# Decoder step on one core: the first projection's tiles, identity products, and the order of weight loads at the output projection

## The chip, the core and the metric

The kernel runs on one core of one Trainium2 chip. The metric is the device time of one execution in microseconds (us), the median of the runs; smaller is better. TensorE does the matrix products (and its weight loads beside them), VectorE (DVE), ScalarE (ACT) and GpSimd (POOL) the elementwise work, SyncE (SP) issues the transfers.

## What is computed

One inference step of a decoder with two layers and width 1024, over a prompt of 2048 tokens and 32 sample tokens (8 sequences of 4) with a paged cache. Layer 0 has an HGRN2 branch (heads "A") and a forgetting-attention branch (heads "B"), layer 1 is GLA (heads "C"). Cut to what matters here:

```python
def rmsnorm(x, g):
    xf = x.astype(jnp.float32)
    y = xf * lax.rsqrt(jnp.mean(xf * xf, axis=-1, keepdims=True) + EPS)
    return (y * g.astype(jnp.float32)).astype(x.dtype)
...
def even_mixer(h, w_in, b_fox, lb, hgrn_gain, w_out, hgrn_s0, fox_attend):
    proj = h @ w_in
    qa, fa, ia, ga, qb, kb, vb, gb, fb = _split(proj, [A_WIDTH] * 4 + [B_WIDTH] * 4 + [B_HEADS])
    ...
    out = jnp.concatenate([o_a, o_b], axis=-1) @ w_out
    return out, s_a, kb_h, vb_h, log_fb
```

The change touches two places of this: `rmsnorm` with `h @ w_in` for the first rows of the prompt, and `... @ w_out` of layer 0.

## The kernel before

Every f32 product is made of f16 halves: an operand is split into a hi and a lo part, and one product is three matrix products, hi by hi, hi by lo and lo by hi (`mm3`, L476 to L480). The prompt goes in two halves of 1024 rows; the first half also carries the 32 sample rows, so it has eight tiles of 128 tokens and one of 32.

**Units of weights.** A projection is cut into units of up to 272 columns of weights. A unit has four steps (`half_unit`, L315): *fetch* loads the raw weights (tiles `wr_*`), *measure* takes the largest absolute value of each of four parts on VectorE (tiles `rm_*`, L292, L294), *scale* spreads it over the partitions with a product against the identity on TensorE (tile `spr_*`, L279) and makes a power of two of it on VectorE, *split* makes the hi and lo weights (`w_*`; ScalarE L345 and L352, VectorE L346, GpSimd L353). `staged` (L1070) calls the products of unit j and, between them, steps of units j+1 to j+3, by a list `todo`. The first unit of layer 0 is "Ai" (values v, products `pt_Av`, tokens on the partitions, 48 products for a pair of tiles), the second "Ag" (gates, products `pf_Ag`, in segments of 352 tokens of 24 products each), the third "Aqf".

**Ahead of the first unit's products** stands the norm (`norm_groups`, L408), for pairs of token tiles. *prep* squares a tile with the sum on ScalarE (L426, `nsq`), takes the mean and its root (VectorE L403 `rst`, GpSimd L405) and scales the tile on VectorE (L428, `nx`). *turn* transposes eight pieces k = 0 to 7 of both tiles on TensorE (L440, `nt`), and `split_evac` evacuates each piece as hi on ScalarE (L473) and lo on VectorE (L474) into `act`. A product of piece k needs both. `handover` (L452) interleaves the pairs' turns with the products of the first unit; in the first half `turn1` prepares pairs 2 and 3. The sample tile's products are a form of their own (`few_rows`, L510): copies `sam` on VectorE (L517), products `pS` (L522), three additions on VectorE (L527). The constants of later steps (`more_consts`) follow on VectorE.

**The order on an engine** is decided when the program is built, by a scheduler; `tc.issue_after(x)` keeps the instructions in its scope behind x. At run time each engine works through its list in order and waits by semaphores.

**The start of the output projection** (`phase_odd`, L1798): the rows y of layer 0 come back from memory in pieces of 256 tokens (`y_pieces`, L1608, tiles `yr`, two buffers), are split into `act` (ScalarE L1628 to L1632, VectorE L1633, GpSimd L1630), and meet four units of weights (`wr_o`, called units 0 to 3 here, products `pt_o`); `row_tiles` (L1859) loads the rows of x that are added.

Notation: L12 is line 12 of the kernel before; `nx_512` is the tile of tokens 512 to 639.

Of the kernel before, what the change touches and what calls it, by code (L numbers as in the profile page):

```python
# [1 line left out]

# [119 lines left out]
class Kern:  # L122
# [134 lines left out]
    def spread(self, x, pps, tag, nm):  # L257

        nc = self.nc
        m, t = self.kcol(), self.kcol()  # L260
        nc.vector.tensor_reduce(m, x, mybir.AxisListType.X, ALU.max, apply_absolute_value=True)
        ps = pps.tile([P, 512], F32, tag=tag, name=f"spr_{nm}")
        nc.tensor.matmul(ps[:, :P], m.to_broadcast([P, P]), self.ident, start=True, stop=True)
        nc.vector.reduce_max(t, ps[:, :P], axis=mybir.AxisListType.X)
        return t
# [141 lines left out]

    def norm_groups(self, pool, pps, act, hf, get_tile, gain, tags=("gr", "o")):  # L408

        nc = self.nc
        tiles = self.ttiles(hf)

        def mk(grp):
            xs, raw = [], []

            def load():
                raw.extend(get_tile(c0, n) for c0, n in grp)

            def prep():
                for j, (c0, n) in enumerate(grp):
# [8 lines left out]
            def turn(at=None, then=None):  # L431
                c0 = grp[0][0]
                if grp[-1][0] == HALF:
                    self.sam = None
                with ExitStack() as st:
                    for k in range(KT):
                        ps = pps.tile([P, 512], F32, tag=tags[k % 2], name=f"nt{c0}_{k}")
                        w = 0
                        for (_, n), xn in zip(grp, xs):
                            nc.tensor.transpose(ps[:, w : w + n], xn[:n, k * P : (k + 1) * P], self.ident[:n, :n])  # L440
                            w += n
                        self.split_evac(ps[:, :w], act[0][:, k, c0 : c0 + w], act[1][:, k, c0 : c0 + w],
                                        gain[:, k : k + 1])
                        if k == at:
                            then(st)

            return prep, turn, load

        return [mk(tiles[g : g + 2]) for g in range(0, len(tiles), 2)]
# [32 lines left out]
    def proj_fm(self, pps, act, W, off, M, hf, evac, nm):  # L482
        for c0, n in self.segs(hf):
            ps = pps.tile([P, 512], F32, tag="pj", name=f"pf_{nm}{c0}")
            for k in range(KT):
                self.mm3(ps[:M, :n], [x[:, k, off : off + M] for x in W],
                         [x[:, k, c0 : c0 + n] for x in act], k == 0, k == KT - 1)
            evac(ps[:M, :n], c0, n)
            yield 24 * (n / 2.4 + 3)

    def proj_tm(self, pps, act, W, hf, evac, nm, width=256, pairs=True):
# [3 lines left out]
        for g in range(0, len(tl), per):  # L495
# [7 lines left out]
            for j, (c0, n) in enumerate(grp):  # L503
                for k in range(KT):
                    self.mm3(ps[:n, j], [x[:, k, c0 : c0 + n] for x in act],
                             [x[:, k, :width] for x in W], k == 0, k == KT - 1)
            evac(ps[:n, : len(grp)], g, len(grp), n)
# [450 lines left out]
    def phase_even(self):  # L958
# [4 lines left out]
        with pool("act", side="right") as ap, pool("w", side="right") as w0, pool("wl", side="right") as wp1, \  # L963
# [30 lines left out]
            for hf in range(2):  # L994
# [10 lines left out]
                lin = lins[hf]  # L1005
                groups = self.norm_groups(nrm, pps, act, hf, get_x, self.g_even)
                first = self.handover(groups, dense(0, 1), last)
                if hf == 0:
# [19 lines left out]
                    turns = [turn0, turn1] + [g[1] for g in groups[2:]]  # L1028
                    first = self.handover(list(zip(steps, turns)), dense(0, 1), last)
                    drain(first)  # L1030
                    with tc.issue_after(self.last_x.ins), tc.issue_after(self.last_a.ins), \
                            tc.issue_after(self.last_v.ins):
                        self.more_consts(wp)
# [36 lines left out]
    def staged(self, us, a, b, beside=None):  # L1070
# [537 lines left out]
    def y_pieces(self, hf, layer, act, pool):  # L1608
# [5 lines left out]
        def mk(c0, dc, s, w, sy):  # L1614
            t = {}

            def load():
                t["raw"] = pool.tile([P, KT, 256], F32, tag="yr", name=f"yr{layer}{hf}{c0}{s}")[:, :, :w]
                nc.sync.dma_start(t["raw"], y[:, :, dc + s : dc + s + w].rearrange("k p t -> p k t"))

# [177 lines left out]
    def phase_odd(self):  # L1798
# [4 lines left out]
        with pool("act2", side="right") as ap, pool("w2", side="right") as w0, pool("yr2", side="right") as y0, \  # L1803
# [197 lines left out]
```

## Time and profile before

| | us |
|---|---|
| median of 3 runs | 2395.92 |
| lowest and highest run | 2392.24, 2399.04 |
| profiled execution | 2394.72 |
| its span in the trace | 2392.4 |
| TensorE busy in it | 2294.1 |
| VectorE, ScalarE, GpSimd busy | 1417.9, 1107.5, 753.7 |

The profile shows one execution. The device time holds the span and 2.3 us around it. The granted TensorE clock was 0.986 of full speed on average. TensorE is busy nearly throughout; the stretches that the change touches are the first 75 us and some 40 us from 1300 us on.

### The profile page before, as it was taken

The page shows a single profiled execution, that of the slowest core. Times are in us where ns is not written, and L with a number is a line of the kernel's source. Part 1 is how long each engine was busy: PE and PEld are TensorE (multiplying, and loading weights), DVE is VectorE, ACT ScalarE, POOL GpSimd, SP SyncE. Part 2 cuts the span into 40 slices and gives each one's busy share as a digit, 9 for nine tenths or more (in the row PEclk, how much of TensorE's full clock was granted, in tenths as well). Part 3 has the DMA queues.
Part 4 walks back from the last instruction along what each step waited for, and adds up shares of the span by engine and source line. Part 5 has one row for each costly group of instructions (what it writes and reads, how often), then busy time and mean ns, then how long its engine had stood idle before and what let it go on. Part 6 is the DMA issues. An engine that isn't in the chain of part 4 may idle for free. (4 is left out here: it accounts for less than half of the span.)

```text
span 2392.4 us, 58667 instructions
## 1 busy us (share of the span) xinstructions
PE 2294.1 (96%) x23324; PEld 1633.7 (68%) x23324; DVE 1417.9 (59%) x3347; ACT 1107.5 (46%) x2458; POOL 753.7 (32%) x843
## 2 busy tenths in 40 slices
PE   6999999999999999999999999999999999999998
PEld 5677677864655875655446876777778766666887
DVE  7566556446655548666767463665675645557554
ACT  5334343342333226556667454535543635545333
POOL 2233222112212225234556211432452222322322
PEclk9999999999999999999999999999999999999999
DMA  6231234535541267676874632122156312114453
GB/s 198 63 88 58 81 113 142 175 92 143 149 136 43 85 192 258 223 251 203 270 241 134 213 109 58 46 81 86 50 151 196 111 41 70 43 59 159 154 192 147
DMA packets 297013, 317.24 MB, mean 133 GB/s; under 512 B 39730, under 2 KB 241011, under 8 KB 296739
## 3 DMA queue, kind: packets, MB, share of 16 engines
q1 hardware_dynamic: 295234, 308.98, 41.1%
q8 instruction: 183, 3.00, 0.5%
q0 software_dynamic: 1504, 4.52, 0.5%
q14 instruction: 92, 0.75, 0.1%
HBM read 242.31 MB, written 71.11 MB: 131 GB/s over the span
## 5 line engine op out<-in xcount | busy, mean ns | idle before, releaser
L480 PE MATMUL pt_o<-w_o,act 128*128 128x256 f16 x1024 | 280.5, 274 | 3.1 <-DVE act L1633 2.9
L478 PE MATMUL pt_o<-w_o,act 128*128 128x256 f16 x1024 | 280.7, 274 | 1.3 <-ACT sg1C L534 1.1
L479 PE MATMUL pt_o<-w_o,act 128*128 128x256 f16 x1024 | 280.5, 274 | 1.0 <-POOL w_o L353 1.0
L480 PEld LDWEIGHTS <-act 128*128 128x128 f16 x2304 | 226.6, 98 | 36.1 <-issue 4.6
L478 PEld LDWEIGHTS <-act 128*128 128x128 f16 x2304 | 226.6, 98 | 36.0 <-ACT act L473 4.0
L479 PEld LDWEIGHTS <-act 128*128 128x128 f16 x2304 | 226.7, 98 | 32.4 <-issue 2.9
L478 PE MATMUL pt_Cv<-w_Cv,act 128*128 128x256 f16 (+1 forms) x512 | 140.3, 275 | 1.7 <-ACT act L473 0.9
L644 POOL TENSOR_TENSOR kA<-kA,fA 128x512 f32<-128x512 f32 (+1 forms) x56 | 79.8, 1425 | 192.6 <-PE gl_A L610 143.0
L479 PE MATMUL pt_Cv<-w_Cv,act 128*128 128x256 f16 (+1 forms) x512 | 140.0, 274 | 0.0
L480 PE MATMUL pt_Cv<-w_Cv,act 128*128 128x256 f16 (+1 forms) x512 | 139.7, 274 | 0.0
L1241 ACT ACTIVATE L<-L,nm,kc 128x512 f32<-128x512 f32 (+3 forms) x160 | 118.2, 741 | 36.9 <-DVE nm L1239 27.2
L644 POOL TENSOR_TENSOR kC<-kC,fC 128x512 f32<-128x512 f32 (+1 forms) x56 | 81.8, 1461 | 148.2 <-PE gl_C L610 101.3
L1249 POOL TENSOR_SCALAR L<-L,nm 128x512 f32<-128x512 f32 (+3 forms) x160 | 98.8, 631 | 70.8 <-DVE nm L1245 28.6
L1276 ACT ACTIVATE th<-pt 128x512 f16<-128x512 f32 (+3 forms) x159 | 80.7, 527 | 59.8 <-PE pt L1269 58.9
L1277 DVE TENSOR_TENSOR tl<-pt,th 128x512 f16<-128x512 f32 (+3 forms) x159 | 94.4, 609 | 20.3 <-ACT th L1276 19.0
L1269 PE MATMUL pt<-ident,L 128*128 128x128 f32 x544 | 91.3, 280 | 4.9 <-DVE tl L1277 2.4
L1269 PEld LDWEIGHTS pt<-ident,L 128*128 128x128 f32 x544 | 66.7, 143 | 32.4 <-DVE tl L1277 9.1
L1393 PEld LDWEIGHTS pkt<-ident,pgcache_fox_k 128*128 128x128 f32 x512 | 58.1, 141 | 44.4 <-issue 25.6
L1393 PE MATMUL pkt<-ident,pgcache_fox_k 128*128 128x128 f32 x512 | 76.1, 279 | 4.7 <-DVE kts L1397 2.0
L478 PE MATMUL pt_Av<-w_Ai,act 128*128 128x256 f16 x256 | 70.9, 277 | 1.9 <-ACT act L473 1.9
L479 PE MATMUL pt_Av<-w_Ai,act 128*128 128x256 f16 x256 | 70.7, 276 | 0.4 <-DVE w_Ai L346 0.4
L478 PE MATMUL pt_Bk<-w_Bk,act 128*128 128x256 f16 x256 | 71.0, 277 | 0.0
(952 smaller groups left out, 6738.3 us busy)
## 6 DMA issues: line engine op xcount, KB each, us to landing
pgcache_fox_k<-in_cache_fox_k SPq DMA_DIRECT2D x128, 256.0 KB, 4.2
pgcache_fox_v<-in_cache_fox_v SPq DMA_DIRECT2D x128, 256.0 KB, 4.2
yr<-yT SPq DMA_DIRECT2D x16, 1024.0 KB, 7.4
nx<-in_x_prompt SPq DMA_DIRECT2D x16, 512.0 KB, 5.4
wr_Aqf<-in_w_in_even SPq DMA_DIRECT2D x64, 128.0 KB, 3.2
wr_o<-in_w_out_even SPq DMA_DIRECT2D x32, 256.0 KB, 4.5
wr_Cv<-in_w_in_odd SPq DMA_DIRECT2D x32, 256.0 KB, 3.8
wr_Cqk<-in_w_in_odd SPq DMA_DIRECT2D x64, 128.0 KB, 2.8
```

The lines of the kernel that those rows point to most:

```text
L478: nc.tensor.matmul(ps, lh[0], rh[0], start=first, stop=False)
L479: nc.tensor.matmul(ps, lh[0], rh[1], start=False, stop=False)
L480: return nc.tensor.matmul(ps, lh[1], rh[0], start=False, stop=last)
L644: nc.gpsimd.tensor_tensor(kv[:, :, 0], kv[:, :, 0], t1.to_broadcast([P, nb, w]), ALU.mult)
L1241: self.last_exp = nc.scalar.activation(lt[:, :w], lt[:, :w], AF.Exp, bias=nm[:, 0:1], scale=ib, accum_out=nm[:, 2 + j : 3 + j])
L1249: nc.gpsimd.tensor_scalar(lt[:, :w], lt[:, :w], nm[:, 1:2], 2.0**14, ALU.mult, ALU.mult)
L1269: nc.tensor.transpose(pt[:, w : w + P], rows[b][s // 4][0][:, (s % 4) * P : (s % 4 + 1) * P], self.ident)
L1276: nc.scalar.activation(th[:, a:w], pt[:, a:w], AF.Copy),
L1277: nc.vector.tensor_tensor(tl[:, a:w], pt[:, a:w], th[:, a:w], ALU.subtract)))
L1393: nc.tensor.transpose(pk[:, j * P : (j + 1) * P], pgs[j][:, h * P : (h + 1) * P], self.ident)
```

## The change

1. In the first half, the squares of the second tile of pairs 1 to 3 (tokens 384, 640 and 896) are made on VectorE, by one operation that multiplies and sums, and no longer on ScalarE.
2. 21 products of the identity with itself, 128x128 in f32 into a PSUM tile that nobody reads, are put ahead of and between the first pair's transposes: nine behind the gain's spread product, four behind the first transpose, one behind each of the eight transposes of the second tile.
3. Pair t+1 is loaded and prepared behind the middle of turn t, for t = 1 to 3; before, pairs 2 and 3 both in turn 1.
4. The first segment of the second unit is issued ahead of the sample rows' products of the first; the third unit is measured during the second instead of during the first, and its scale step is put behind the last product issued.
5. At the output projection, the row loads from the third on and the loads of units 2 and 3 stand behind the last piece of y.

```diff
+    def norm_groups(self, pool, pps, act, hf, get_tile, gain, tags=("gr", "o"), share=False):
...
-                    nc.scalar.activation(sq[:n], xt[:n], AF.Square, accum_out=ss[:n])
+                    if share and j and c0 > P:
+                        nc.vector.tensor_tensor_reduce(sq[:n], xt[:n], xt[:n], 1.0, 0.0, ALU.mult, ALU.add, ss[:n])
+                    else:
+                        nc.scalar.activation(sq[:n], xt[:n], AF.Square, accum_out=ss[:n])
...
+            warm = pps.tile([P, 512], F32, tag="st", name="warm")
+            def warm_up(n, after):
+                with tc.issue_after(after.ins):
+                    for _ in range(n):
+                        nc.tensor.matmul(warm[:, :P], self.ident, self.ident, start=True, stop=True)
+            warm_up(9, self.last_spread)
...
-                    def turn0():
-                        groups[0][1](1, lambda st: st.enter_context(tc.issue_after(self.last_scale.ins)))
-                    def turn1():
-                        groups[1][1](KT // 2 - 1, lambda st: behind(self.last_a, 2))
-                        behind(self.last_a, 3)
-                    steps = [lambda: None, lambda: behind(self.last_split, 1), lambda: None, lambda: None, groups[4][0]]
-                    turns = [turn0, turn1] + [g[1] for g in groups[2:]]
-                    first = self.handover(list(zip(steps, turns)), dense(0, 1), last)
+                    def each0(st, k, j):
+                        if j or k == 0:
+                            warm_up(1 if j else 4, self.last_t)
+                        if (k, j) == (2, 0):
+                            st.enter_context(tc.issue_after(self.last_scale.ins))
+                    def turn0():
+                        groups[0][1](each0)
+                    def turn(t):
+                        groups[t][1](lambda st, k, j: behind(self.last_a, t + 1) if (k, j) == (KT // 2, 0) else None)
+                    steps = [lambda: None, lambda: behind(self.last_split, 1), lambda: None, lambda: None, lambda: None]
+                    turns = [turn0] + [lambda t=t: turn(t) for t in (1, 2, 3)] + [groups[4][1]]
+                    first = dense(0, 1)
+                    drain(self.handover(list(zip(steps, turns)), islice(first, 4), last))
+                    gates = dense(1, 3)
+                    next(gates)
                     drain(first)
...
-                drain(dense(1, 3))
+                drain(dense(1, 3) if hf else gates)
...
+                    if n == 2:
+                        st.enter_context(self.tc.issue_after(self.last_mm.ins))
                     self.ready[u] = us[u][0][n]()
...
-            if j:
+            if j == 1 and beside:
+                todo = [[], [(2, 1), (4, 0)], [(2, 2)], [(2, 3), (3, 1)], [(3, 2)], [(3, 3)]]
+            elif j:
                 todo = [[(j + 3, 0), (j + 2, 1)], [(j + 2, 2)], [(j + 2, 3)]]
             elif beside is None:
                 todo = [[(2, 0), (1, 3)], [(3, 0)], [(2, 3)]]
             else:
-                todo = [[(1, 0)], [(1, 1)], [(2, 0), (1, 2), (1, 3)], [(3, 0)], [(2, 1), (2, 2), (2, 3)]]
+                todo = [[(1, 0)], [(1, 1)], [(2, 0), (1, 2), (1, 3)], [(3, 0)]]
...
-                    nc.sync.dma_start(t[:m], self.rows(hf, c0, m, first))
+                    with ExitStack() as st:
+                        if first and j > 1:
+                            st.enter_context(tc.issue_after(self.last_yr.ins))
+                        nc.sync.dma_start(t[:m], self.rows(hf, c0, m, first))
...
-            with tc.issue_after(self.last_y.ins):
+            with tc.issue_after(self.last_y.ins), tc.issue_after(self.last_yr.ins):
                 drain(dense(0, 3))
```

`last_mm`, `last_t`, `last_spread` and `last_yr` are the last such instruction issued. The changed file's line numbers lie some lines higher: its L478 and L477 are the lo and hi evacuations, L432 the scaling, L428 VectorE's square, L482 to L484 the three products.

**TensorE around the third unit's scale product.** `pS_Av` are the sample rows' products, `pf_Ag` the second unit's. Before:

```order
L522 MATMUL pS_Av_683<-w_Ai_153,sam_Av_680 32x256
L279 MATMUL spr_Aqf_721<-ident,rm_Aqf_715 128x128
L478 LDWEIGHTS w_Ag_577
L478 MATMUL pf_Ag_847<-act,w_Ag_577 128x352
L479 LDWEIGHTS w_Ag_577
```

After the change the scale product has left this place; in front of it stand three segments of the second unit, the first of them ahead of the sample rows' products:

```order
L484 MATMUL pf_Ag_913<-act,w_Ag_599 128x352
L280 MATMUL spr_Aqf_942<-ident,rm_Aqf_902 128x128
L482 LDWEIGHTS w_Ag_599
L482 MATMUL pf_Ag_951<-act,w_Ag_599 128x352
L483 LDWEIGHTS w_Ag_599
```

`pf_Ag_913` is the third segment and `pf_Ag_951` the fourth; before, all six came behind the first scale product.

**VectorE during pair 1's turn.** `act<-nt_k` is the lo evacuation of piece k, `rst` the mean of squares, `nx` the scaling of a tile. Before:

```order
L474 SCALAR_TENSOR_TENSOR act<-nt_3_241,g_even,act 128x256
L403 TENSOR_SCALAR rst_n_249<-nss_247 128x1
L428 TENSOR_SCALAR nx_512_166<-nx_512_166,rsr_n_251 128x1024
L474 SCALAR_TENSOR_TENSOR act<-nt_4_262,g_even,act 128x256
L261 TENSOR_REDUCE kc<-g_odd 128x1
L474 SCALAR_TENSOR_TENSOR act<-nt_5_267,g_even,act 128x256
L403 TENSOR_SCALAR rst_n_257<-nss_255 128x1
L474 SCALAR_TENSOR_TENSOR act<-nt_6_272,g_even,act 128x256
L428 TENSOR_SCALAR nx_640_168<-nx_640_168,rsr_n_259 128x1024
L474 SCALAR_TENSOR_TENSOR act<-nt_7_277,g_even,act 128x256
```

After:

```order
L478 SCALAR_TENSOR_TENSOR act<-nt_3_263,g_even,act 128x256
L404 TENSOR_SCALAR rst_n_273<-nss_271 128x1
L428 ISA nsq_278,nss_279<-nx_640_178 128x1024
L428 ISA nss_279 128x1
L478 SCALAR_TENSOR_TENSOR act<-nt_4_268,g_even,act 128x256
L262 TENSOR_REDUCE kc<-g_odd 128x1
L432 TENSOR_SCALAR nx_512_176<-nx_512_176,rsr_n_275 128x1024
L478 SCALAR_TENSOR_TENSOR act<-nt_5_289,g_even,act 128x256
L478 SCALAR_TENSOR_TENSOR act<-nt_6_294,g_even,act 128x256
L404 TENSOR_SCALAR rst_n_281<-nss_279 128x1
L478 SCALAR_TENSOR_TENSOR act<-nt_7_299,g_even,act 128x256
L432 TENSOR_SCALAR nx_640_178<-nx_640_178,rsr_n_283 128x1024
```

The square of tile 640 (the two rows `ISA`) stands behind the step that reads ScalarE's sum of tile 512, and ahead of the lo evacuation of piece 4.

**SyncE at the output projection.** `wr_o_19432` is unit 1, `wr_o_19542` and `wr_o_19611` are units 2 and 3; `yr` are the pieces of y of tokens 512, 768 and the sample rows. Before:

```order
L327 DMA wr_o_19432<-in_w_out_even 128x2x256 x4
L327 DMA wr_o_19542<-in_w_out_even 128x2x256
L1619 DMA yr_19437<-yT_76 128x8x256
L327 DMA wr_o_19542<-in_w_out_even 128x2x256 x3
L327 DMA wr_o_19611<-in_w_out_even 128x2x256 x4
L1619 DMA yr_19449<-yT_76 128x8x256
L1619 DMA yr_19461<-yT_76 128x8x32
```

After:

```order
L328 DMA wr_o_19454<-in_w_out_even 128x2x256 x4
L1646 DMA yr_19459<-yT_76 128x8x256
L1893 DMA row_0_19495<-in_x_prompt 128x1024
L1646 DMA yr_19471<-yT_76 128x8x256
L1893 DMA row_1_19497<-in_x_prompt 128x1024
L688 DMA s_C_21834<-in_state_gla 128x2x256
L688 DMA s_C_21836<-in_state_gla 128x2x256
L1646 DMA yr_19483<-yT_76 128x8x32
L1893 DMA row_2_19499<-in_x_prompt 128x1024
```

Seven more row loads follow there, and only then the eight loads of units 2 and 3.

## Rows read from the trace of the kernel before

**Rows 1.** Page, part 1: engine, busy us, share of the span, instructions

```profile
PE 2294.1 (96%) x23324; PEld 1633.7 (68%) x23324; DVE 1417.9 (59%) x3347; ACT 1107.5 (46%) x2458; POOL 753.7 (32%) x843
```

**Rows 2.** Waits of TensorE, 0 to 75 us: waiting line, releaser, total, times, longest

```profile
PE spr_Aqf L279 <- DVE kc L261: 6.8, 1, 6.8
PE nt L440 <- DVE nx L428: 5.2, 2, 3.8
PE pS_Av L522 <- DVE sam_Av L517: 1.5, 1, 1.5
```

**Rows 3.** Windows: length, busy (count) of PE, PEld, DVE, ACT, POOL, clock, DMA share, GB/s

```profile
52.40:59.10 6.70, 0.00 (x0) 0.00 (x0) 6.29 (x18) 0.98 (x2) 0.01 (x1) 0.50 0.48 145
59.10:64.00 4.90, 4.86 (x17) 2.79 (x18) 4.74 (x16) 0.32 (x3) 1.95 (x6) 0.50 0.00 0
```

**Rows 4.** Timeline of TensorE: start, duration, line, output and inputs

```profile
19.69 0.29 PE L480 MATMUL pt_Av<-w_Ai,act 128*128 128x256 f16 x1
...
23.71 0.28 PE L478 MATMUL pt_Av<-w_Ai,act 128*128 128x256 f16 x1
...
33.41 0.27 PE L478 MATMUL pt_Av<-w_Ai,act 128*128 128x256 f16 x1
...
41.87 0.27 PE L478 MATMUL pt_Av<-w_Ai,act 128*128 128x256 f16 x1
...
48.69 0.27 PE L480 MATMUL pt_Av<-w_Ai,act 128*128 128x256 f16 x1
...
72.68 0.31 PE L480 MATMUL pf_Ag<-act,w_Ag 128*128 128x352 f16 x1
72.83 0.31 PE L478 MATMUL pf_Ag<-act,w_Ag 128*128 128x352 f16 x1
...
83.57 0.31 PE L478 MATMUL pf_A00f<-act,w_Aqf 128*128 128x352 f16 x1
```

**Rows 5.** Timeline of ScalarE in the first pair of the first unit

```profile
23.18 1.57 ACT L473 ACTIVATE act<-nt,g_even 128x256 f16<-128x256 f32 x4 [4.12 <-PE nt L440]
24.62 1.07 ACT L426 ACTIVATE nsq<-nx 128x1024 bf16<-128x1024 f32 x1
...
25.66 0.85 ACT L817 ACTIVATE v<-pt_Av,kc 128x256 f32<-128x256 f32 x2
```

**Rows 6.** Timeline of VectorE, same stretch and ahead of it

```profile
17.69 0.88 DVE L474 SCALAR_TENSOR_TENSOR act<-nt,g_even,act 128x256 f16<-128x256 f32 x2
...
25.82 0.15 DVE L403 TENSOR_SCALAR rst_n<-nss 128x1 f32<-128x1 f32 x1 [0.47 <-ACT nsq L426]
...
29.20 0.75 DVE L428 TENSOR_SCALAR nx<-nx,rsr_n 128x1024 f32<-128x1024 f32 x1
29.87 0.48 DVE L474 SCALAR_TENSOR_TENSOR act<-nt,g_even,act 128x256 f16<-128x256 f32 x1
```

**Rows 7.** Tile views of fx and yr: durations ns min/median/max, first and last start, forms

```profile
L1829 DVE SCALAR_TENSOR_TENSOR fx<-fx,rsr_f,gb x9: 1272/1285/1286, 2305.4 to 2380.2; 128x1024 f32<-128x1024 f32 x8, 32x1024 f32<-32x1024 f32 x1
L1633 DVE SCALAR_TENSOR_TENSOR act<-yr,kc,act x54: 275/746/1986, 1294.5 to 2311.9; 128x512 f16<-128x512 f32 x48, 128x64 f16<-128x64 f32 x6
```

**Rows 8.** Timeline of VectorE behind the sample rows' copies

```profile
50.73 2.45 DVE L292 TENSOR_REDUCE rm_Aqf<-wr_Aqf 128x1 f32<-128x512 f32 x4
...
56.08 2.39 DVE L292 TENSOR_REDUCE rm_Aqf<-wr_Aqf 128x1 f32<-128x512 f32 x4
...
63.52 0.42 DVE L527 TENSOR_TENSOR few_Av<-few_Av,pS_Av 32x256 f32<-32x256 f32 x1
```

**Rows 9.** Timeline of GpSimd: the first split of the third unit

```profile
67.88 2.31 POOL L353 TENSOR_TENSOR w_Aqf<-wr_Aqf,w_Aqf 128x512 f16<-128x512 f32 x2 [0.94 <-ACT w_Aqf L352]
```

**Rows 10.** Timeline of TensorE at the output projection's second unit

```profile
1333.10 0.27 PE L479 MATMUL pt_o<-w_o,act 128*128 128x256 f16 x1 [0.28 <-POOL w_o L353]
...
1335.32 0.27 PE L479 MATMUL pt_o<-w_o,act 128*128 128x256 f16 x1 [0.75 <-POOL w_o L353]
```

**Rows 11.** Timeline of SyncE's DMA queue at the output projection

```profile
1319.25 5.72 SPq L1863 DMA_DIRECT2D row<-in_x_prompt  x8
```

More of the change, by code (lines that the diff above doesn't have):

```diff
@@ L1 @@
 from contextlib import ExitStack
+from itertools import islice
 import concourse.bass as bass
@@ L262, in spread @@
         ps = pps.tile([P, 512], F32, tag=tag, name=f"spr_{nm}")
-        nc.tensor.matmul(ps[:, :P], m.to_broadcast([P, P]), self.ident, start=True, stop=True)
+        self.last_spread = nc.tensor.matmul(ps[:, :P], m.to_broadcast([P, P]), self.ident, start=True, stop=True)
         nc.vector.reduce_max(t, ps[:, :P], axis=mybir.AxisListType.X)
@@ L406, in rstd @@
         return r
-    def norm_groups(self, pool, pps, act, hf, get_tile, gain, tags=("gr", "o")):
+    def norm_groups(self, pool, pps, act, hf, get_tile, gain, tags=("gr", "o"), share=False):
         nc = self.nc
@@ L429, in prep, with turn @@
                     xs.append(xt)
-            def turn(at=None, then=None):
+            def turn(each=None):
                 c0 = grp[0][0]
@@ L438, in turn @@
                         w = 0
-                        for (_, n), xn in zip(grp, xs):
-                            nc.tensor.transpose(ps[:, w : w + n], xn[:n, k * P : (k + 1) * P], self.ident[:n, :n])
+                        for j, ((_, n), xn) in enumerate(zip(grp, xs)):
+                            self.last_t = nc.tensor.transpose(ps[:, w : w + n], xn[:n, k * P : (k + 1) * P], self.ident[:n, :n])
                             w += n
+                            if each:
+                                each(st, k, j)
                         self.split_evac(ps[:, :w], act[0][:, k, c0 : c0 + w], act[1][:, k, c0 : c0 + w],
                                         gain[:, k : k + 1])
-                        if k == at:
-                            then(st)
             return prep, turn, load
@@ L485, in proj_fm @@
             for k in range(KT):
-                self.mm3(ps[:M, :n], [x[:, k, off : off + M] for x in W],
-                         [x[:, k, c0 : c0 + n] for x in act], k == 0, k == KT - 1)
+                self.last_mm = self.mm3(ps[:M, :n], [x[:, k, off : off + M] for x in W],
+                                        [x[:, k, c0 : c0 + n] for x in act], k == 0, k == KT - 1)
             evac(ps[:M, :n], c0, n)
@@ L504, in proj_tm @@
                 for k in range(KT):
-                    self.mm3(ps[:n, j], [x[:, k, c0 : c0 + n] for x in act],
-                             [x[:, k, :width] for x in W], k == 0, k == KT - 1)
+                    self.last_mm = self.mm3(ps[:n, j], [x[:, k, c0 : c0 + n] for x in act],
+                                            [x[:, k, :width] for x in W], k == 0, k == KT - 1)
             evac(ps[:n, : len(grp)], g, len(grp), n)
@@ L1005, in phase_even @@
                 lin = lins[hf]
-                groups = self.norm_groups(nrm, pps, act, hf, get_x, self.g_even)
+                groups = self.norm_groups(nrm, pps, act, hf, get_x, self.g_even, share=hf == 0)
                 first = self.handover(groups, dense(0, 1), last)
@@ L1018, in behind @@
                             groups[g][0]()
-                    def turn0():
-                        groups[0][1](1, lambda st: st.enter_context(tc.issue_after(self.last_scale.ins)))
-                    def turn1():
-                        groups[1][1](KT // 2 - 1, lambda st: behind(self.last_a, 2))
-                        behind(self.last_a, 3)
-                    steps = [lambda: None, lambda: behind(self.last_split, 1), lambda: None, lambda: None, groups[4][0]]
-                    turns = [turn0, turn1] + [g[1] for g in groups[2:]]
-                    first = self.handover(list(zip(steps, turns)), dense(0, 1), last)
+                    def each0(st, k, j):
[3 more added lines that the diff above has]
+                            st.enter_context(tc.issue_after(self.last_scale.ins))
+                    def turn0():
+                        groups[0][1](each0)
[7 more added lines that the diff above has]
+                    next(gates)
                     drain(first)
+                    first = iter(())
                     with tc.issue_after(self.last_x.ins), tc.issue_after(self.last_a.ins), \
@@ L1618, in load @@
                 t["raw"] = pool.tile([P, KT, 256], F32, tag="yr", name=f"yr{layer}{hf}{c0}{s}")[:, :, :w]
-                nc.sync.dma_start(t["raw"], y[:, :, dc + s : dc + s + w].rearrange("k p t -> p k t"))
+                self.last_yr = nc.sync.dma_start(t["raw"], y[:, :, dc + s : dc + s + w].rearrange("k p t -> p k t"))
             def split(k):
```

## The prediction

> **What bounds the kernel now.** I first read the busy shares: TensorE works 96% of the span [rows 1], so time can only come back where it stands idle, or where it runs at the lower of its two clock levels. Then I read the waits of TensorE in the first 75 us, the only stretch that the first three parts of the change touch. One wait is larger than all others: the first scale product of the third unit stands 6.8 us for a VectorE chain, and the sample rows' products wait another 1.5 us [rows 2]. [...]
>
> [...] Pair by pair, the first unit's products begin at 23.71, 33.41 and 41.87 and the last starts at 48.69 [rows 4]: 9.7, 8.5 and 6.9 us for 48 products of 0.109 us and 16 transposes of about 0.11, 7.0 us of TensorE work. The first two pairs are paced by the chain through ScalarE and VectorE, the last by TensorE itself.
>
> **The change part by part.** I walk the new order with durations of these rows.
>
> *First tiles.* In the old run the products go from half to full pace at 19.69, where the duration falls from 0.42 to 0.29 us [rows 4]. If the identity products raise the clock before 14.8, the first tile could end much sooner, but it needs the lo halves of k = 6 and 7. These ran from 17.69 [rows 6]; now the square of tile 384 is ahead of them on VectorE, so they end near 19.8. The first tile ends at about 19.8, not 20.1. The clock is thus worth 0.3 us there. The second tile's 24 products (2.6 us), the transposes and the two v evacuations, which now stand ahead of the next pair's hi evacuations on ScalarE, put the first hi of pair 1 at about 23.8, where it was 23.18 [rows 5].
>
> *The square.* No row shows VectorE squaring with a sum. Nearest: a VectorE operation with two f32 sources and the same 128x1024 takes 1.285 us [rows 7]. Below, 0.75 us, the one-source scaling of the same tile [rows 6]; above, 3.4 us, if it is stretched as L1633 is at worst (1986 against 746 ns, x2.7) [rows 7]. I take 1.28, by the row with the same sources, plus 0.08 for reading the sum. ScalarE's own square is 1.07 us [rows 5], so one tile's square costs more on VectorE; the gain can only be that two run side by side. But in the new order they don't: VectorE's square follows the step that waits for ScalarE's sum, so it starts when that ends.
>
> [...]
>
> *One turn of a pair,* from its first hi to the next pair's: four hi 1.44 us, ScalarE's square until its rst starts 1.20 (24.62 to 25.82) [rows 5, 6], rst 0.07, VectorE's square 1.36, a lo 0.39 (two take 0.88, and the second adds about 0.4), a scaling 0.67, two lo 0.78, rst 0.07, the last lo 0.47 [rows 6]: 6.45 us. Then the second tile's 24 products, 2.62, and 0.15 + 0.73 us for the v evacuations [rows 5]. Together 9.95 us. The same reading checks on the old run: the last lo of pair 1 ends at 30.35, plus 2.62 is 32.97, and pair 2 started at 33.41. The old pair 2 took only 8.5 us because its tiles had been squared a pair earlier; the change fetches and squares pair t+1 only in turn t, so it gives that lead away. First hi of pair 2 at 33.75, of pair 3 at 43.7, its last lo (the second unit's split lies between) at 51.15; with 24 products and the sample tile's transposes the first unit ends at about 55.5, 6.6 us later than before.
>
> *The second unit's first segments.* They now stand ahead of the scale product. One segment (22 products of 0.149 left: 3.3 us) ends at 58.9, the sample products at 60.3, two more segments at 67.5. Meanwhile VectorE does the sample copies, then what it did before: eight maxima (2.4 us for four), the constants (2.9 us between the two groups of maxima) [rows 8], the short steps. That is 9.8 us from the copies' end at about 56.6: the scale product is ready at 66.4, before TensorE gets there. The fourth segment also needs the buffer that the third sample addition frees; this addition comes 1.5 us later than the maxima (it ended at 63.9 in the old run) [rows 8], at about 67.9. So the fourth segment starts at about 68.0. It was the product at 72.83 that began it before [rows 4]. Gain: about 4.8 us; I take 4.5 because some transposes of the sample tile may stall singly. The third unit's split is the next that could be late: POOL ended it at 70.19 [rows 9] and its first use was at 83.57 [rows 4], 13.4 us of cover. Now the scale product comes 8.4 us later and the use 4.8 us earlier, which leaves 0.2 us: I cost it at nothing, but every us by which it is later still is a us of stall, and I allow 2 us for it in the range.
>
> *Output projection.* TensorE stalls there 0.28 and 0.75 us for the split of the second unit of weights [rows 10]. The seven loads of the third and fourth unit that stood ahead of the y piece of tokens 768 now go behind the pieces, so pieces and the second unit's split should come some us sooner: gain 1.0 us, at least 0, at most these two stalls. The price would be paid by the third unit's weights: the eight row loads left SP by 1325 [rows 11], the weights follow, and even 12 us from there to landing is 1337. They are first used when the second unit, begun at 1333.10, is through: 8 tiles of 24 products of 0.109 us and the sample rows' 24, about 1356. The order inside attention shifts a little too: 0, with bounds of 2 us either way, an estimate by the size of the projection's stalls taken twice.
>
> *Identity products.* 21 of them, each at most the 0.4 us of a half-pace product, 13 of them before the first tile's transposes are through, where TensorE waited 3.8 and 1.4 us for the scaled tiles [rows 2]: hidden. If the clock does not rise, the eight single ones delay the first scale product by some 1.4 us.
>
> Sum: 4.5 + 1.0 = 5.5 us less than the profiled execution's 2394.72 us, 2389.2. That execution lies 1.2 us under the median of the runs (2395.92, from 2392.24 to 2399.04), so against the median I forecast 2390.5 us. What a measurement here can tell from no change is 0.3%, 7.2 us: the forecast is a true gain that lies inside this bound.
>
> **Rivals.**
> 1. *The pairs run as fast as TensorE allows.* For it: pair 3 took 6.9 us. Against: the turn above. If turns are 8.5 us, as the old pair 2, the front gains 2.9 us more, 2387.5; at 7.0 the first unit ends at 49.5, the fourth segment starts near 62 and the whole prize comes back: gain 10.9 + 1.0, 2384. Chance 0.27.
> 2. *The identity products do not raise the clock* where it is wanted, and the change does not do what it says there: 1.4 us later scales and 0.3 us of clock lost, 2392. For it: the transposes of 8 to 14 us did not raise it before. Chance 0.08.
> 3. [...] Chance 0.16.
> 4. *Slower: VectorE's square is stretched.* Two sources of f32 at 128x1024 beside POOL and transfers that write the same memory; L1633 shows x2.7 at worst. At 3.4 us each turn grows by 2.1, three by 6.4: the front gives back all of its 4.5 and 1.9 more, 2397 after the projection's gain. It decides from a square of about 3.1 us on. Against it: it needs the worst case three times, and L1829 ranges from 1272 to 1286. Chance 0.07.
>
> **How the numbers follow.** The forecast case has 0.42 (its own range 2388 to 2394), the rivals 0.27, 0.08, 0.16 and 0.07. Over 0.3% faster means under 2388.7: nearly all of rival 1 and about a quarter of the forecast case, 0.35. Slower by over 0.3% means above 2403.1: a part of rival 4 with the spread of the runs, 0.05. The rest, 0.60, is within. The range reaches from rival 1's far end less a little, 2383, to rival 4, 2398.
>
> **What would show it.** [...] Wrong: pairs 7 to 8.5 us apart (rival 1), squares above 2 us (rivals 3 and 4), half pace of the products after 14.8 (rival 2), or a new wait of TensorE behind the sample additions, with the fourth segment after 70 us.

## The result, and the profile after

The changed kernel is slower: 2400.74 us median of 19 runs (2398.63 to 2405.97), against 2395.53 us (2386.62 to 2399.63, 19 runs) before. The ratio is 1.0027, interval 1.0019 to 1.0036, about 6.5 us (the medians alone lie 5.2 us apart). The forecast was 2390.5 us in a range up to 2398, and slower by over 0.3% had a chance of 0.05. Slower by 0.27% lies within the 0.3% that the forecast called "no change", but above the range, and on the wrong side.

The front did become shorter. The first lines are the page's span and busy share of TensorE after the change, then its waits of the first 75 us (waiting line, releaser, us in total, times, longest):

```profile
span 2397.2 us, 58751 instructions
PE 2295.4 (96%) x23366; PEld 1636.5 (68%) x23366; DVE 1418.8 (59%) x3353; ACT 1104.5 (46%) x2452; POOL 756.5 (32%) x843
```

```profile
PE pt_Av L482 <- ACT act L477: 3.4, 4, 1.2
PE pt_Av L484 <- DVE act L478: 3.2, 3, 1.3
PE nt L444 <- DVE nx L432: 2.7, 4, 0.9
...
PE pf_Ag L482 <- DVE few_Av L531: 0.7, 1, 0.7
```

The waits of 6.8 us for the scale product and of 1.5 us for the sample copies [rows 2] are gone. In their place stand some ten short waits inside the pairs. The windows (length, busy time and count of TensorE, of its weight loads, of VectorE, ScalarE and GpSimd, granted clock, DMA share, GB/s) answer to [rows 3]:

```profile
52.40:59.10 6.70, 6.70 (x39) 4.15 (x40) 2.35 (x13) 2.41 (x10) 3.12 (x5) 0.76 0.50 152
59.10:64.00 4.90, 4.90 (x53) 3.11 (x52) 4.58 (x10) 1.27 (x4) 0.00 (x0) 1.00 0.13 31
64.00:73.00 9.00, 8.26 (x57) 5.41 (x56) 8.45 (x28) 3.70 (x11) 4.86 (x15) 1.00 0.00 1
```

TensorE works where it stood, though at a mean clock of 0.76 from 52.4 to 59.1. To see what is left of this later, I took the start of every ScalarE, VectorE and GpSimd instruction that two traces share, and subtracted: minus is earlier than in the kernel before. Medians over 80 us, the start of the stretch at the left:

```
        again  changed  shift  after_lay  old_prep  best  gates_lay
 160    -0.31    -1.75   0.14     -0.78     -9.10  -7.57    -10.75
 800    -3.22    -0.55   3.30     -0.85     -4.75  -9.60    -12.03
 960    -3.56     2.68   7.08     -2.77     -1.17  -9.30    -15.08
1520    -1.51     2.70   9.69      0.11     -2.45 -12.25    -12.98
2320    -1.21     5.13   6.98      4.11      2.19  -5.85     -8.87
```

The columns beside "changed" are the runs below; "again" is the kernel before, traced a second time. So the front gave 1.75 us, not 4.5 (front_only below, with the same front, shows 0.4 there, so one trace tells it to about 1.5 us). Then the changed kernel loses 3.2 us between 800 and 960, where the diff touches nothing. Two executions of one program drift by some 3 us too, so a single difference of that size needs a reason of its own. This one has it. VectorE at the start of the attention, before (two of its first score tiles L):

```profile
886.66 0.41 DVE L1233 CUSTOM_DVE_ANT_0 L<-s,cb 128x256 f32<-128x256 f32 x1
...
887.91 0.56 DVE L1233 CUSTOM_DVE_ANT_0 L<-s,cb 128x384 f32<-128x384 f32 x1
```

and after, where the bracket names an idle time and what ended it:

```profile
888.63 0.42 DVE L1260 CUSTOM_DVE_ANT_0 L<-s,cb 128x256 f32<-128x256 f32 x1 [2.39 <-DMA vd<-Bv]
...
891.17 0.56 DVE L1260 CUSTOM_DVE_ANT_0 L<-s,cb 128x384 f32<-128x384 f32 x1 [1.36 <-DMA vd<-Bv]
```

VectorE waits 2.39 and 1.36 us for the store `vd<-Bv` before it may write a score tile. No such wait was there before. TensorE stands behind it:

```profile
890.61 0.69 PE L1296 MATMUL pt<-ident,L 128*128 128x128 f32 x2 [2.88 <-POOL L L1276]
```

The windows of 20 us from 880, before and after, show 16.49 and 12.66 us of TensorE work at the same clock:

```profile
880.00:900.00 20.00, 16.49 (x84) 9.12 (x83) 11.18 (x50) 9.32 (x24) 10.91 (x18) 0.74 0.96 320
```

```profile
880.00:900.00 20.00, 12.66 (x65) 6.64 (x64) 9.10 (x40) 7.50 (x18) 9.93 (x16) 0.74 1.02 338
```

In the built programs the reason can be read. Scratch memory is laid out in them by the first use of each tag. The change asks for the gates' tile (tag th, two buffers) ahead of the sample rows' tile (tag c2, four buffers), and so exchanges their places; the values Bv lie in c2, and the attention's tiles later take the same memory:

```
             before             changed
c2 buffers   113504 .. 121695   117600 .. 125791
Bv114        117600             121696 .. 123743
L, 3rd tile  123392 .. 125439   123392 .. 125439
```

The numbers are bytes of a partition. The third score tile now overlaps Bv114, whose store is still under way; before it lay clear of all Bv. The fourth (121344 .. 123391 in both programs) overlaps Bv114 too after the change.

### The profile page after: what moved, and what is told of

The parts are those of the page before. It is cut to its first block, busy times and chain, and to the rows that moved or that the text cites. A ratio compares the mean times of both kernels' runs of the same rounds, so it can differ in the third digit from the quotient of the medians.

```text
span 2397.2 us, 58751 instructions
## 1 busy us (share of the span) xinstructions
PE 2295.4 (96%) x23366; PEld 1636.5 (68%) x23366; DVE 1418.8 (59%) x3353; ACT 1104.5 (46%) x2452; POOL 756.5 (32%) x843
## 5 line engine op out<-in xcount | busy, mean ns | idle before, releaser
L484 PE MATMUL pt_o<-w_o,act 128*128 128x256 f16 x1024 | 280.0, 273 | 3.6 <-DVE act L1660 3.6
L482 PE MATMUL pt_o<-w_o,act 128*128 128x256 f16 x1024 | 280.1, 274 | 1.6 <-ACT sg1C L538 1.6
L484 PEld LDWEIGHTS <-act 128*128 128x128 f16 x2304 | 226.3, 98 | 39.3 <-DVE act L478 4.5
L482 PEld LDWEIGHTS <-act 128*128 128x128 f16 x2304 | 226.2, 98 | 39.2 <-ACT act L477 7.3
L482 PE MATMUL pt_Cv<-w_Cv,act 128*128 128x256 f16 (+1 forms) x512 | 140.3, 275 | 1.7 <-ACT act L477 0.9
L484 PE MATMUL pt_Cv<-w_Cv,act 128*128 128x256 f16 (+1 forms) x512 | 139.7, 274 | 0.0
L482 PE MATMUL pt_Av<-w_Ai,act 128*128 128x256 f16 x256 | 70.4, 275 | 4.9 <-ACT act L477 4.9
L484 PE MATMUL pt_Av<-w_Ai,act 128*128 128x256 f16 x256 | 70.4, 276 | 3.2 <-DVE act L478 3.2
L482 PE MATMUL pt_Bk<-w_Bk,act 128*128 128x256 f16 x256 | 71.0, 277 | 0.0
```

The source lines that it names most:

```text
L482: nc.tensor.matmul(ps, lh[0], rh[0], start=first, stop=False)
L484: return nc.tensor.matmul(ps, lh[1], rh[0], start=False, stop=last)
```

## The experiments

Three theories went in. A, refined to O after the first four runs: the scheduler, whose own reckoning of time (its clock, not TensorE's) the front's parts shift, puts the attention phase in another order (it does, on TensorE, VectorE, ScalarE and GpSimd), and that costs the time. B: the loads at the projection cost it. C: drift. When the wait above was found, L joined them: the place in memory costs it. Every run is given as a ratio to the kernel before on the same chip, with its interval.

**again.** No edit.

> The kernel before, unchanged, once more, for a second trace: how far do two executions of the same program drift apart along the span? All theories expect the same time (ratio 1.000 within 0.15%). If the change's loss is only drift between executions (theory C), this trace drifts from the first by 2 us or more from 90 us on, in jumps at the same places as the changed kernel (near 887, 1760 and 1860 us). If the order of the work sets the loss (theories A and B), it drifts by less than 1.5 us there and the wait at 887 us is not seen.

Measured: 1.0001 (0.9988 to 1.0015). Its trace drifts from the first by up to 4.3 us, with a jump of 3.9 us near 360 us, where the granted clock was half for 10.2 us in the first execution and did not fall in the second. The wait at 887 us is not there, and between 800 and 960 it moves by 0.3 us only. The expectation of less than 1.5 us of drift was too narrow; the absence of the wait speaks against C.

**front_only**

```diff
-            with tc.issue_after(self.last_y.ins), tc.issue_after(self.last_yr.ins):
+            with tc.issue_after(self.last_y.ins):
...
-                        if first and j > 1:
+                        if False:
```

> The changed kernel with the old order of loads at the output projection: parts 1 to 4 of the change alone. Theory A (the parts at the front gain some 1.7 us there, but the scheduler, whose clock they shift, puts the attention phase in another order, and that costs 3 to 8 us): about as slow as the changed kernel, 4 to 7 us over the kernel before. Theory B (the loads at the projection cost the time): 1 to 3 us faster than the kernel before. Theory C (drift): within 2 us of the kernel before.

Measured: 1.0020 (1.0006 to 1.0035), 4.8 us slower. The loss is in parts 1 to 4, as A expects.

**proj_only.** The kernel before with the three edits of part 5 alone.

```diff
+                self.last_yr = nc.sync.dma_start(t["raw"], ...)
...
+                        if first and j > 1:
+                            st.enter_context(tc.issue_after(self.last_yr.ins))
...
+            with tc.issue_after(self.last_y.ins), tc.issue_after(self.last_yr.ins):
```

> The kernel before with part 5 alone, the loads at the output projection. The attention phase keeps its old order on every engine. Theory A: within 2 us of the kernel before. Theory B: 4 to 8 us slower than the kernel before, with a stall or a fall of the clock near 1310 us. Theory C: within 2 us.

Measured: 1.0001 (0.9987 to 1.0014). B falls. TensorE's stalls of 0.28 and 0.75 us [rows 10] are gone in this trace, but no shorter time is seen. The trace of front_only, with the old loads, shows no such stall either, so the loads aren't the only thing that moves it.

**old_prep**

```diff
-                        groups[t][1](lambda st, k, j: behind(self.last_a, t + 1) if (k, j) == (KT // 2, 0) else None)
+                        if t != 1:
+                            return groups[t][1]()
+                        groups[1][1](lambda st, k, j: behind(self.last_a, 2) if (k, j) == (KT // 2, 0) else None)
+                        behind(self.last_a, 3)
...
-                    steps = [..., lambda: None]
+                    steps = [..., groups[4][0]]
```

> The changed kernel, but pairs 2 and 3 are prepared in turn 1 as before (part 3 undone). This gives the second pair its lead back, and the attention phase stands in nearly the old order. Theory A: front 4 to 7 us shorter than before, and no loss in the attention: 3 to 7 us faster than the kernel before. Theory B: the front's gain less 4 to 8 us, so -2 to +4 us. Theory C: 3 to 6 us faster.

Measured: 0.9980 (0.9967 to 0.9993), 4.8 us faster than before and some 11 us faster than the change. At the front it gains 9.1 us, so part 3 costs 7.3 us there beside the changed kernel's trace (8.7 beside front_only's). But between 800 and 960 it loses 3.6 us, although it has nearly the old order in the attention: A alone can't say why. The wait of VectorE for the store is in it too (us in total, times, longest):

```profile
DVE L L1263 <- DMA vd<-Bv: 4.1, 2, 2.7
```

**shift.** The kernel before, with the two tags in pools of their own, c2 above th:

```diff
+        with ..., pool("wl", side="right") as wp1, pool("wlt", side="right") as wpt, \
-            wp = Pool(..., Pool(wp1, {"c2": EC2, "th": ETH}))
+            wp = Pool(..., Pool(wp1, {"c2": EC2}), Pool(wpt, {"th": ETH}))
```

> The kernel before with nothing moved in the order of any engine; only the memory places of two scratch tags, c2 and th, are exchanged, so that the four c2 buffers lie 4096 bytes higher, as they do in the changed kernel (there because the gates' th tile is now asked for before the sample rows' c2 tile). In the trace of the changed kernel the third score tile L of the attention then lies on a buffer whose values Bv are still being stored. Theory L (this place costs the time): a wait of VectorE for the store vd, 3 to 4 us in all near 886 us, and 2 to 4 us slower than the kernel before (ratio 1.001 to 1.0017). Theory O (the order that the scheduler gave the attention costs it): no change, ratio 1.000 within 0.0012.

Measured: 1.0017 (1.0004 to 1.0030), 4.1 us slower, with not one instruction moved. The wait appears, on the same tiles:

```profile
892.73 0.42 DVE L1233 CUSTOM_DVE_ANT_0 L<-s,cb 128x256 f32<-128x256 f32 x1 [2.61 <-DMA vd<-Bv]
...
895.28 0.56 DVE L1233 CUSTOM_DVE_ANT_0 L<-s,cb 128x384 f32<-128x384 f32 x1 [1.37 <-DMA vd<-Bv]
```

**after_lay.** The changed kernel with the same edit, but `wlt` opened ahead of `wl`, which gives c2 its old place.

```diff
-        with ..., pool("wl", side="right") as wp1, \
+        with ..., pool("wlt", side="right") as wpt, pool("wl", side="right") as wp1, \
```

> The changed kernel with nothing moved in the order of any engine; only the two scratch tags lie where they lay before. Theory L: the wait of VectorE for the store at 886 us is gone and it is 3 to 5 us faster than the changed kernel, so 1 to 3 us over the kernel before; if the layout is the whole loss, 1.7 us under it. Theory O: as slow as the changed kernel, 5 to 7 us over the kernel before.

Measured: 1.0008 (0.9993 to 1.0023), 1.9 us over the kernel before; the change had 6.5. The wait is gone:

```profile
885.76 0.41 DVE L1260 CUSTOM_DVE_ANT_0 L<-s,cb 128x256 f32<-128x256 f32 x1
...
886.86 0.56 DVE L1260 CUSTOM_DVE_ANT_0 L<-s,cb 128x384 f32<-128x384 f32 x1
```

Together the two runs show L from both sides: by the ratios the place costs 4.1 us (shift) and 4.6 us (the change less after_lay), each good to 3 or 4 us. The traces are steadier. By the same reckoning as in the table above, the four kernels in which Bv114 lies in the way (the change, front_only, old_prep, shift) all wait 3.8 to 4.1 us for this store and come out 3.2 to 3.8 us later between the stretches at 800 and at 960. The nine other traces have no such wait, and there they move between 3.3 us earlier and 0.3 us later. after_lay also speaks against O: every engine has exactly the order of the changed kernel, and it gains 1.9 us in this stretch.

**best.** old_prep and after_lay together; later texts call it the mended kernel.

> Both mendings together: the changed kernel with pairs 2 and 3 prepared in turn 1 as before, and the scratch tags where they lay before. Theory L: the front's 9 us stay, the wait at 886 us is gone: 7 to 10 us faster than the kernel before (ratio 0.9958 to 0.997). Theory O: as the run with the old preparation alone, 4 to 6 us faster (ratio 0.9975 to 0.9983).

Measured: 0.9956 (0.9939 to 0.9973), 2386.48 us median of 6 runs beside 2394.82 before (10.5 us by the ratio, 8.3 by the medians). It is the number that L expected, and faster than the kernel before and the changed one.

**share_only.** The kernel before with part 1 alone.

```diff
+                    if share and j and c0 > P:
+                        nc.vector.tensor_tensor_reduce(sq[:n], xt[:n], xt[:n], 1.0, 0.0, ALU.mult, ALU.add, ss[:n])
...
```

> The kernel before with part 1 alone: the second tiles' squares on VectorE. The places in memory stay, but the scheduler puts the attention phase in the same other order as in the changed kernel. The wait of 6.8 us for the scale product stays, so the front itself should move by less than 2 us. Theory L: within 2 us of the kernel before. Theory O: 3 to 7 us slower, lost between 880 and 1300 us.

Measured: 1.0004 (0.9991 to 1.0018). Its front is 1.9 us later. Its order in the attention is near the changed kernel's, though not the same: of 938 VectorE instructions there 103 stand out of the old order, as in the changed kernel, and 30 differ between the two. The loss is absent: with after_lay, O falls as far as these intervals reach. The square itself, in this run and in the change (tile view, ns min/median/max):

```profile
L428 DVE CUSTOM_DVE_ANT_0 nsq<-nx x3: 1212/1215/1216, 17.7 to 37.3; 128x1024 bf16<-128x1024 f32 x3
```

The last four runs ask which part earns the gain: part 4 by itself (theory P4), or the parts together (theory PA).

**gates_lay.** The kernel before with part 4 alone, and c2 in its old place by the pools of after_lay.

```diff
+                    gates = dense(1, 3)
+                    next(gates)
...
-                drain(dense(1, 3))
+                drain(dense(1, 3) if hf else gates)
...
+            if j == 1 and beside:
+                todo = [[], [(2, 1), (4, 0)], [(2, 2)], [(2, 3), (3, 1)], [(3, 2)], [(3, 3)]]
...
```

> The kernel before with part 4 alone (the gates' first segment ahead of the sample products, the third unit measured during the second), with the scratch tags where they lay. Squares, identity products, preparation and the loads at the projection stay as before. Theory P4 (this reorder is the whole gain): the first unit ends near 49 us as before, the fourth segment starts near 62 us, and it is 8 to 11 us faster than the kernel before. Theory PA (the parts need one another: without identity products and squares on VectorE the first unit ends later or the clock falls): 3 to 6 us faster.

Measured: 0.9958 (0.9942 to 0.9974), 2382.59 us median of 6 runs beside 2393.09. This is P4's number: the reorder of the units alone gives what best gives, each good to some 4 us. Its order in the attention is about as far from the old one as the changed kernel's (93 of 938 VectorE instructions), which is one more point against O. TensorE's timeline in this run:

```profile
53.14 0.84 PE L523 MATMUL pS_Av<-w_Ai,sam_Av 128*32 128x256 f16 x24
61.40 0.46 PE L280 MATMUL spr_Aqf<-ident,rm_Aqf 128*128 128x128 f32 x2 [0.15 <-DVE rm_Aqf L295]
```

```profile
61.88 0.31 PE L479 MATMUL pf_Ag<-act,w_Ag 128*128 128x352 f16 x1
```

The sample products come at 53.14, the scale product waits 0.15 us instead of 6.8 [rows 2], and the fourth segment starts at 61.88, where it was 72.83 [rows 4].

**best_nw**

```diff
-                    for _ in range(n):
+                    for _ in range(0):
```

> The mended kernel (old preparation, old places of the scratch tags) without the 21 identity products; they take nothing from the result. Theory P4: 0 to 1 us slower than the mended kernel, so 8 to 10 us faster than the kernel before; the products run at half pace from 14.8 to 19.7 us again, but the first tile ends as before, by its lo halves. Theory PA: 2 to 4 us slower than the mended kernel.

Measured: 0.9956 (0.9942 to 0.9970). The identity products earn nothing that can be seen; without them the window from 14 is half paced again (25 instructions in 5.06 us), as P4 says. The clock in that row reads 1.00 all the same; the pace shows in the single products, 0.42 us up to 18.67 and 0.27 from 19.08:

```profile
14.00:19.50 5.50, 5.06 (x25) 3.55 (x26) 5.50 (x12) 4.07 (x8) 1.46 (x1) 1.00 1.09 360
```

```profile
18.67 0.42 PE L482 MATMUL pt_Av<-w_Ai,act 128*128 128x256 f16 x1
...
19.08 0.27 PE L484 MATMUL pt_Av<-w_Ai,act 128*128 128x256 f16 x1
```

The order in the attention isn't best's here (103 of 935 VectorE instructions there stand elsewhere), so a difference of a few us could hide in it.

**best_ns.** The squares back on ScalarE in the kernel of best.

```diff
-                groups = self.norm_groups(..., share=hf == 0)
+                groups = self.norm_groups(..., share=False)
```

> The mended kernel with all squares on ScalarE. Theory P4: the squares on VectorE give nothing or cost 1 to 2 us at the front (part 1 alone cost 1.9 us there), so 9 to 12 us faster than the kernel before. Theory PA: 2 to 4 us slower than the mended kernel.

Measured: 0.9975 (0.9965 to 0.9985), 6.0 us faster than before. That is 4.5 us behind best, as PA said, but its front came out 10.4 us ahead, as P4 said, and the intervals of the two runs touch. Its order in the attention differs from best's as well (106 of 935). What the squares are worth stays open.

**best_old_loads**

```diff
-            with tc.issue_after(self.last_y.ins), tc.issue_after(self.last_yr.ins):
+            with tc.issue_after(self.last_y.ins):
...
-                        if first and j > 1:
+                        if False:
```

> The mended kernel with the old order of loads at the output projection. Part 5 alone moved the time by nothing that could be measured: within 1.5 us of the mended kernel, 8 to 11 us faster than the kernel before. If part 5 is worth the 1.0 us that the prediction gave it, it is 1 us slower than the mended kernel, and the stall of TensorE for the second unit's split near 1327 us is back.

Measured: 0.9977 (0.9964 to 0.9989), 5.5 us faster than before, where 8 to 11 were expected. The stall for the second unit's split is back:

```profile
PE pt_o L483 <- POOL w_o L354: 1.4, 2, 0.8
```

The interval overlaps with best's interval, and part 5 alone moved nothing; whether the loads earn a few us there stays open.

## Why the prediction was wrong

**The step that failed is the term for everything outside the touched places.** The prediction put the order inside attention at 0, with 2 us either way, an estimate by the projection's stalls that no row of the attention bore out, and it never looked at the places of tiles in memory. The exchange of c2 and th costs 4.1 to 4.6 us there (shift, after_lay): VectorE waits 2.39 and 1.36 us for a store. With this term the sum would have been about 1 us faster instead of 5.5, still on the wrong side. The rest of the miss of 12 us is in the sizes of other terms: the front, put at 4.5 us, gave 1.75 in its trace; the projection, put at 1.0, gave nothing that proj_only could measure; 3.6 us stay open.

**The pairs' turns were a little too short.** Forecast 9.95 us each, first hi of the pairs at 23.8, 33.75 and 43.7. ScalarE after the change:

```profile
23.86 1.57 ACT L477 ACTIVATE act<-nt,g_even 128x256 f16<-128x256 f32 x4
...
33.81 0.84 ACT L821 ACTIVATE v<-pt_Av,kc 128x256 f32<-128x256 f32 x2 [5.89 <-PE pt_Av L484]
34.54 1.57 ACT L477 ACTIVATE act<-nt,g_even 128x256 f16<-128x256 f32 x4
...
44.81 1.57 ACT L477 ACTIVATE act<-nt,g_even 128x256 f16<-128x256 f32 x4
```

So 10.68 and 10.27. The chain was right: the square begins behind ScalarE's sum, and the next hi waits for the v evacuation (33.81), which waits for the last product. The square was 1.22 us and not 1.28:

```profile
26.57 1.22 DVE L428 CUSTOM_DVE_ANT_0 nsq<-nx 128x1024 bf16<-128x1024 f32 x1
27.71 0.08 DVE L428 DVE_READ_ACCUMULATOR2_ANT nss<- 128x1 f32 x1
...
30.16 0.47 DVE L478 SCALAR_TENSOR_TENSOR act<-nt,g_even,act 128x256 f16<-128x256 f32 x1
```

The last lo ended at 30.63, 6.77 us after the pair's first hi, against 6.45. From there to the v evacuation it took 3.18 us, not 2.77: 26 products and one transpose of the next pair still ran, where the forecast had 24 products. The loss against the old pair 2 was foreseen in kind; its price, 7.3 us at the front, is shown by old_prep.

**The end of the first unit was 3.1 us too early in the forecast.** I had about 55.5; its last product starts at 58.33 and ends at 58.60. The turns had cost 1.1 us of this (44.81 against 43.7). Behind waits of TensorE of 0.56, 1.23 and 0.43 us from 48.6 to 51.4 the granted clock then fell to 0.50 for 3.4 us, which no step had:

```profile
52.75 0.42 PE L482 MATMUL pt_Av<-w_Ai,act 128*128 128x256 f16 x1
...
55.45 0.39 PE L484 MATMUL pt_Av<-w_Ai,act 128*128 128x256 f16 x1
55.67 0.28 PE L482 MATMUL pt_Av<-w_Ai,act 128*128 128x256 f16 x1
...
58.33 0.27 PE L484 MATMUL pt_Av<-w_Ai,act 128*128 128x256 f16 x1
```

From 52.4 to 55.4 the granted clock is 0.50 and the products of 0.42 us start 0.21 us apart; from 55.6 to 58.6 it is 0.99, and those of 0.27 us start 0.11 apart. By these paces some 1.7 us are lost over the 3.4 us, an estimate; the last 0.3 us aren't traced to a cause. The sample additions follow: the third was forecast to end at 67.9 and ends at 70.83, 2.1 us of this by the copies' end (58.7 against 56.6). As forecast, the fourth segment waits for it:

```profile
70.41 0.42 DVE L531 TENSOR_TENSOR few_Av<-few_Av,pS_Av 32x256 f32<-32x256 f32 x1
```

```profile
70.89 0.31 PE L482 MATMUL pf_Ag<-act,w_Ag 128*128 128x352 f16 x1 [0.74 <-DVE few_Av L531]
```

So it starts at 70.89, not 68.0, against 72.83 before: the 1.9 us that are left of 4.8. A fourth segment after 70 us, behind the sample additions, was one of the prediction's own signs of being wrong. The third unit's split, costed at nothing, held: TensorE shows no wait for it up to 120 us.

**The square's rivals.** Rivals 3 and 4, with chances of 0.16 and 0.07, needed squares above 2 us. No run shows one: in the changed kernel three squares took 1212 to 1216 ns each, 0.06 us under the 1.28 us that the forecast took from row L1829. The trace shows the operation as a custom form, with 0.08 us behind it for reading the sum. Rival 2 fell too: the first product behind the identity products, at 14.50, took 0.27 us; before, the first one, at 14.82, took 0.42.

**The projection.** Stalls of 1.0 us were to go, and they went (no wait of TensorE for a split is left there). No time came back in proj_only. In the changed kernel the clock fell for 3.4 us at 1312 (0.50 from 1311.8 to 1315.1, with products of 0.42 us), behind two waits in the attention's end. In front_only, with the old loads, it fell for 3.4 us at 1314, so the loads aren't the cause:

```profile
1310.67 0.27 PE L482 MATMUL fo<-th,h_v 128*128 128x256 f16 x1 [1.36 <-ACT th L1303]
...
1311.63 0.27 PE L483 MATMUL fo<-tl,h_v 128*128 128x256 f16 x1 [0.69 <-DVE tl L1304]
```

**What stays open.** The change costs 6.5 us. The front gives 1.75 back in its trace, the layout takes 4.6 (after against after_lay); 3.6 us are left, with after_lay's own interval of 3.6 us either way. Small waits of TensorE downstream differ mostly by some tenths (from 90 to 860 us 2.8 against 2.6 us for `scT`, 1.5 against 1.3 for `act`); between the two executions of the kernel before, GpSimd's wait for VectorE differs by as much (7.5 against 7.3 from 872 to 900). One wait is larger: in the changed kernel TensorE stands 1.2 us for VectorE, which itself has waited for a load of rows `xo`:

```profile
1868.40 0.75 DVE L1697 SCALAR_TENSOR_TENSOR xo<-pt_o,kc,xo 128x512 f32<-128x512 f32 x1 [2.18 <-DMA xo<-in_x_prompt]
```

```profile
1869.60 0.44 PE L444 MATMUL nt<-ident,x1r 128*128 128x128 f32 x2 [1.22 <-DVE y_C L597]
```

The two traces of the kernel before don't have it; neither does after_lay, which has the changed kernel's order. best has it with 2.6 us and is faster all the same. Whether it is a further cause or chance, no run here settles.

Rival 1 had the first unit end at 49.5, the fourth segment start near 62 and the time at 2384. gates_lay comes out so (the last product starts at 49.01, the segment at 61.88, 10.95 us ahead of the 72.83 before [rows 4], where the rival counted 10.9), but not by faster pairs: it leaves them as they were. The prediction gave the rival 0.27 and never asked which parts worked against it.

## What to carry to other kernels

Price the parts of a change one by one, each in the order that the others leave: here one part earned some 10 us by itself, one cost 7 at the front, two (the identity products, the loads) earned nothing that was seen for certain, and what the squares are worth stayed open. When tags or tiles are asked for in another order, compare the addresses of the two built programs, not only the order of the instructions: a new wait for a store can turn up hundreds of us later (here 2.39 and 1.36 us, near 890 us). And before a loss of a few us is explained, trace the unchanged kernel twice.

## What the runs showed of the hardware

Two executions of one program drifted by up to 4.3 us along the span. The largest jump, 3.9 us, lies where the clock of TensorE fell in the one and not in the other (10.2 us at half clock from 364 us on, before; none there in again). VectorE squared and summed 128x1024 f32 in 1.22 us, against a median of 1.06 us on ScalarE; reading the sum took 0.08 and 0.19 us more. In the kernel before, the products of 352 columns started 0.29 us apart from 59.73 to 63.84, at a granted clock of 0.50, and 0.15 us apart from 72.5 to 73.2, at 1.00. In the changed kernel the first nine identity products took 3.99 us, the next four 1.06:

```profile
4.09 3.99 PE L982 MATMUL warm<-ident 128*128 128x128 f32 x18
...
8.37 1.06 PE L982 MATMUL warm<-ident 128*128 128x128 f32 x8
...
14.50 0.27 PE L482 MATMUL pt_Av<-w_Ai,act 128*128 128x256 f16 x1
```

The 18 instructions of the first group started 0.21 us apart (4.09 to 7.72), the next eight 0.11 (8.37 to 9.26). So TensorE ran at full pace from about 8 us on and was still there at the first unit's products at 14.5, with identity products among the transposes between; without them, in best_nw, products took 0.42 us up to 18.67, and full pace came at 19.1 us. Even so, no difference in the time of the kernel was seen.
